# Group two's FFN: downs in seven products, sums of up weights stored ahead, squares of h moved

## The chip, the cores and the metric

The kernel runs on one core of a Trainium2 chip. The metric is the device time of one execution in microseconds; where several runs stand, the median counts. A core has five engines that run side by side, each with a queue of its own in program order: TensorE (PE), VectorE (DVE), ScalarE (ACT), GpSimd (POOL) and SyncE (SP), which only issues transfers. An instruction waits on semaphores for what it needs from other engines; all behind it in its queue wait with it.

## The reference

One layer of an encoder with two attention mixers and an FFN, for 1056 tokens (1024 of a prompt, 32 of a running stream), all in float32. The part that the change touches, cut down:

```python
h = x + jnp.einsum('bld,de->ble', m, w_out)
u = jnp.einsum('bld,df->blf', rmsnorm(h, g_ffn), w_up)        # 1024 -> 4096
return h + jnp.einsum('blf,fd->bld', jnp.square(jax.nn.relu(u)), w_down)
```

rmsnorm divides h by the root of the mean of its squares; since relu(u)^2 only scales with the square of that factor, the kernel uses h unscaled for the ups and multiplies the result by 1/(mean of squares + eps) at the end.

## The kernel before, in words

**Tiles.** Activations lie with channels on the 128 partitions and tokens along the columns. Each float32 operand is split in a high part, rounded to the fast matmul format, and the rest (`xh`, `xl`; `wh`, `wl`), and a block of 128x128 weights takes three matmuls (`three`: high times high, high times rest, rest times high). A *unit* is a 256 KB tile of weights, 128x512, four such blocks. For each unit SyncE loads `wst`, ACT casts it to `wh`, and POOL subtracts to get `wl` (`unit`, L435; three buffers for `wst`, five for each of the pair).

**Groups and stages.** The tokens are two groups: group one with 512, group two with 544 in two column halves of 272. Projections and most of the attention come first; then group one's output projection (`out`, L1325) and FFN (`ffn_group`, L1441: 16 ups, 32 downs by quarters `q` of the 4096 channels). Beside FFN one runs "late" attention of group two, which loads k, q and v of each head from DRAM (`k<-dk`, `q<-dq`, `v<-dv`). From about 1300 us on comes group two alone: branches, `out`, FFN two to the end.

**FFN two.** Its ups are already done by a seven-product scheme (Strassen's kind): two ups of 128 channels, two halves of the 1024 inputs and two halves of the columns make a 2x2 by 2x2 block product, which takes seven products of 12 matmuls of 128x272 instead of eight (`go_up_quad`, L1464). It needs four sums of weight tiles (`s1` to `s4`), made in FFN two itself: `quad_units` (L1389) loads a tile with SyncE and adds another one to it by an accumulating transfer, which only POOL's queue issues (four per quad, `raw<-w_up` on POOLq). The sums of h needed (`g.sums`) are made in `out`. The products add up in PSUM banks `pj`, DVE and ACT combine them, square the relu, and split the result. Downs are plain: `go_down` (L1511) takes one unit and two halves of 12 matmuls each into banks `pd`; DVE adds each to `y`. A quad of ups (84 matmuls) and four downs (96) take turns.

**Squares.** `out` also makes the sum of squares of h: for each of 8 row blocks ACT squares it, and POOL adds it to `acc` (L1345 to 1350); `scales` (L1446) sums that over partitions by a matmul with `ones` right after the first ups.

**Order.** All instructions are recorded first (`Plan.record`, L279), and a planner with a cost model then sets the order of each engine by rank and readiness (L353 to 416); all are issued at L410, so every row of the profile has that one line, and one tells groups apart by tile names and shapes.

Of the kernel before, what the change touches and what calls it, by code (L numbers as in the profile page):

```python
# [9 lines left out]
F32 = mybir.dt.float32  # L10
# [92 lines left out]
class Plan:  # L103
# [175 lines left out]
    def record(self, eng, fn, op, args, kw):  # L279
# [52 lines left out]
        if eng == SP and self.hold is not None:  # L332
            deps.add(self.hold)
# [85 lines left out]
class Layer:  # L419
# [77 lines left out]
    def run(self):  # L497
# [34 lines left out]
        self.dh = dt([KB, 128, T], "dh")  # L532

# [104 lines left out]
        self.ffn_group(g2)  # L638
# [640 lines left out]
    def begin_group(self, g, side):  # L1279
        nc, i = self.nc, g.i  # L1280
        g.pool = nc.open(f"g{i}", side)
        if i:
            g.h = nc.tile(g.pool, [128, KB, g.w], F32R, f"gh{i}")
            g.l = nc.tile(g.pool, [128, KB, g.w], F32R, f"gl{i}")
        g.y = nc.tile(g.pool, [128, KB, g.w], F32, f"y{i}")
        g.acc = [nc.tile(g.pool, [128, g.n], F32, f"acc{i}{c}") for c in range(len(g.chunks))]
        g.tmp = lambda name, tag, bufs: nc.tile(g.pool, [128, g.n], F32, name, tag=tag, bufs=bufs)
# [101 lines left out]
    def quad_units(self, f):  # L1389

        nc, a, w = self.nc, self.a, self.quads
        with nc.rank(PREP):
            src = lambda i, j: a["w_up"][f + i, j]

            def load(*blocks, out=None):
                st = out
                if out is None:
                    st = nc.tile(w, [128, 512], F32, "raw", bufs=10)
                    nc.sync.dma_start(st, src(*blocks[0]))
                    blocks = blocks[1:]  # L1400
                for b in blocks:
                    nc.gpsimd.dma_start(st, src(*b), accum_op=ALU.add)
                return st

            def part(z, pool, tag, bufs, eng):
                h = nc.tile(pool, [128, 512], F32R, tag + "h", bufs=bufs)
                l = nc.tile(pool, [128, 512], F32R, tag + "l", bufs=bufs)
                nc.scalar.copy(h, z)
                eng.tensor_sub(l, z, h.bitcast(F32))
                return h, l  # L1410

            V, G = nc.vector, nc.gpsimd
            z = load((1, 0), (1, 1))
            z3 = load((0, 0), (1, 0))
            a11, a22, a12 = load((0, 0)), load((1, 1)), load((0, 1))
            s1 = part(z, w, "s", 4, V)
            load((0, 0), out=z)
            s2 = part(z, w, "s", 4, V)
            load((0, 1), out=z)
            s3 = part(z3, w, "s", 4, V)  # L1420
            s4 = part(z, w, "s", 4, G)
            p11 = part(a11, self.wpool, "w", WB, G)
            p12 = part(a12, self.wpool, "w", WB, G)
            p22 = part(a22, self.wpool, "w", WB, G)
        return p11, p12, p22, s1, s2, s3, s4

    def square(self, g, ps, uh, ul, sign=1.0):

        nc = self.nc
        r = g.tmp("ru", "pb", 3)  # L1430
        nc.scalar.activation(r, ps, AF.Relu, scale=sign)
        if not g.i:
            nc.gpsimd.tensor_mul(r, r, r)
            nc.scalar.copy(uh, r)
            nc.vector.tensor_sub(ul, r, uh.bitcast(F32))
            return
        nc.vector.scalar_tensor_tensor(ps, ps, sign, r, op0=ALU.mult, op1=ALU.mult)
        nc.scalar.copy(uh, ps)
        nc.vector.tensor_sub(ul, ps, uh.bitcast(F32))

    def ffn_group(self, g, late=iter(())):  # L1441
        nc, a, i = self.nc, self.a, g.i
        n = g.n
        rb2 = g.acc

        def scales():  # L1446

            for c in range(len(g.chunks)):
                ps = self.bank("pj")
                nc.tensor.matmul(ps[:, :n], self.ones, g.acc[c], start=True, stop=True)  # L1450
                with nc.rank(FAST):
                    v = g.tmp("rv", "pb", 3)
                    nc.vector.tensor_scalar(v, ps[:, :n], 1.0 / D, EPS, op0=ALU.mult, op1=ALU.add)
                    nc.vector.reciprocal(rb2[c], v)

        nq, us = DFF // 512, {}

        def go_up(f):
            units = [self.unit(a["w_up"][f, j]) for j in range(2)]
            us[f] = uh, ul = g.mh[:, f % 8], g.ml[:, f % 8]  # L1460
            self.column_block(units, lambda k, cs: (g.h[:, k, cs], g.l[:, k, cs]),
                              lambda c, cs, ps: self.square(g, ps, uh[:, cs], ul[:, cs]), g.chunks)

        def go_up_quad(f):  # L1464

            a11, a12, a22, s1, s2, s3, s4 = self.quad_units(f)
            for i in range(2):
                us[f + i] = g.mh[:, (f + i) % 8], g.ml[:, (f + i) % 8]
            ta, tb, tc, td = ([(th[:, k], tl[:, k]) for k in range(4)] for th, tl in g.sums)
            x = lambda j, c: [(g.h[:, 4 * j + k, c * n:c * n + n], g.l[:, 4 * j + k, c * n:c * n + n]) for k in range(4)]  # L1470

            def product(w, xs, ps=None):
                first = ps is None
                if first:
                    ps = self.bank("pj")[:, :n]
                with nc.rank(FILL):
                    for k in range(4):
                        ks = slice(k * 128, k * 128 + 128)
                        self.three(ps, w[0][:, ks], w[1][:, ks], *xs[k], first and k == 0, k == 3, skip_group_check=True)
                return ps  # L1480

            def keep(ps):
                t = nc.tile(self.op, [128, g.w], F32, "part", tag="o32", bufs=4)[:, :n]
                with nc.rank(FAST):
                    nc.scalar.copy(t, ps)
                return t

            def done(i, c, out, ps, more=None):
                cs = slice(c * n, c * n + n)
                uh, ul = us[f + i]  # L1490
                with nc.rank(FAST):
                    if more is not None:
                        nc.vector.tensor_add(out, ps, more)
                    self.square(g, out, uh[:, cs], ul[:, cs], -1.0 if i else 1.0)

            px = product(a11, x(0, 0))
            p1 = keep(px)
            pz = product(s1, ta)
            p5 = keep(pz)
            product(s2, tb, px)  # L1500
            u2 = keep(px)
            product(s4, x(1, 1), pz)
            done(0, 1, pz, pz, u2)
            py = product(a12, x(1, 0))
            done(0, 0, py, py, p1)
            product(s3, tc, px)
            done(1, 1, self.bank("pj")[:, :n], px, p5)
            product(a22, td, px)
            done(1, 0, px, px)

        def go_down(e, q):  # L1511
            units = [self.unit(a["w_down"][e, q])]

            def done(c, cs, ps):
                y = g.y[:, e, cs]
                if q == 0:
                    nc.scalar.copy(y, ps)
                    return
                if q < nq - 1:
                    nc.vector.tensor_add(y, ps, y)  # L1520
                    return
                if e < KB // 2:
                    nc.vector.tensor_add(ps, ps, y)
                    y = hx_of(e, cs)
                nc.vector.tensor_mul(ps, ps, rb2[c])
                nc.vector.tensor_add(g.y[:, e, cs], ps, y)
                nc.sync.dma_start(self.o["yT"][:, e, slice(g.lo + cs.start, g.lo + cs.stop)], g.y[:, e, cs])

            if q == nq - 1 and e >= KB // 2:
                for c, cs in enumerate(g.chunks):  # L1530
                    y = g.y[:, e, cs]
                    nc.gpsimd.tensor_mul(y, y, rb2[c])
                    nc.gpsimd.tensor_add(y, y, hx_of(e, cs))
            self.column_block(units, lambda k, cs: (us[4 * q + k][0][:, cs], us[4 * q + k][1][:, cs]), done, g.chunks,
                              kn=4, tag="pd" if g.i else "pj")

        def hx_of(e, cs):

            return g.h.bitcast(F32)[:, e, cs]

        def reload():

            with nc.rank(PREP):
                nc.sync.dma_start(g.h.bitcast(F32), self.dh[:, :, g.lo:g.lo + g.w].rearrange("e p t -> p e t"))
# [14 lines left out]
        if g.i:  # L1559
            go_up_quad(0)  # L1560
            scales()
            go_up_quad(2)
            for q in range(nq):
# [103 lines left out]
```

## Time and profile before

| | us |
|---|---|
| runs | 1767.86, 1769.7, 1771.3 (median 1769.7) |
| profiled execution, its own time | 1771.3 |
| its span in the trace | 1769.5 |
| start of FFN two | about 1393 |
| last matmul | 1765.5 |
| mean granted clock of TensorE | 0.999 |

Tile names: `gh`, `gl` are h times the norm's gain in its two parts; `xh`, `xl` sums or results that were split; `sh`, `sl` split weight sums; `ru` relu; `part` a kept partial product; `acc` the sum of squares. A row of a group of instructions gives its line, engine, operation, tiles and shapes, the count, busy time and mean nanoseconds of one, then the engine's idle time ahead of them and what ended it.

### The profile page before, as it was taken

The numbers are of one execution on the slowest core, as the hardware profiler recorded it, in microseconds if no ns is written. First come the engines' busy times: TensorE is split into PE (matmuls) and PEld (weight loads), VectorE is DVE, ScalarE is ACT, GpSimd is POOL, SyncE is SP. The second block draws the span as 40 slices with busy tenths as digits, with TensorE's granted clock in tenths as the row PEclk, the third lists the DMA queues.
The fourth block names the chain that finished last, engine by engine and source line by source line (L and its number), as shares of the span: only waits on it lengthen the run. The fifth ranks groups of instructions, "written<-read, shape, count | busy, mean of one in ns | idle before, by whom it ended". The sixth has DMA issues, their size and how long they took to land.

```text
span 1769.5 us, 32605 instructions
## 1 busy us (share of the span) xinstructions
PE 1741.2 (98%) x11394; PEld 1599.9 (90%) x11394; DVE 1050.6 (59%) x2284; ACT 976.5 (55%) x2153; POOL 1046.0 (59%) x909
## 2 busy tenths in 40 slices
PE   8999999999999999999999999999999999999999
PEld 7999999999889888988888888888899999999998
DVE  7555578999655644888755455222347843444445
ACT  7444598983255776766665555533236654444441
POOL 3623232435366575999864555665759966666555
PEclk9999999999999999999999999999999999999999
DMA  7243451444566668556344453533486576666634
GB/s 255 74 133 117 116 177 59 147 144 143 178 173 169 177 183 228 172 177 179 100 135 127 125 144 96 156 101 96 155 262 191 153 169 150 151 153 156 154 68 137
DMA packets 169908, 264.53 MB, mean 149 GB/s; under 512 B 28944, under 2 KB 58224, under 8 KB 169744
## 3 DMA queue, kind: packets, MB, share of 16 engines
q1 hardware_dynamic: 160096, 245.33, 47.3%
q0 software_dynamic: 9216, 16.78, 5.9%
q8 instruction: 90, 1.47, 0.4%
q14 instruction: 74, 0.61, 0.1%
q10 hardware_dynamic: 432, 0.34, 0.1%
HBM read 207.87 MB, written 54.40 MB: 148 GB/s over the span
## 4 chain that ended last, share of the span: by engine, by line
PE 85%; DMA 4%; POOL 4%; DVE 3%; issue 2%; ACT 1%; SPq 1%; ACTq 0%; POOLq 0%; DVEq 0%
PE pj L410 52%; PE s L410 13%; PE pd L410 11%; PE t L410 5%; PE o L410 5%; POOL wl L410 1%; DMA wst<-w_ba 1%; SPq L410 1%; DVE xl L410 1%; POOL xl L410 1%; POOL pb L410 1%; POOL acc L410 0%; DMA raw<-w_up 0%; DMA wst<-w_g 0%; DMA xt<-x 0%
## 5 line engine op out<-in xcount | busy, mean ns | idle before, releaser
L410 POOL TENSOR_TENSOR wl<-wst,wh 128x512 fp32r<-128x512 f32 x350 | 485.7, 1395 | 357.2 <-ACT wh L410 324.6
L410 PE MATMUL pj<-xh,wh 128*128 128x512 f32 (+1 forms) x1600 | 557.2, 349 | 0.7 <-DVE vt L410 0.3
L410 PE MATMUL pj<-xh,wl 128*128 128x512 f32 (+1 forms) x1600 | 557.5, 349 | 0.0
L410 PE MATMUL pj<-xl,wh 128*128 128x512 f32 (+1 forms) x1600 | 555.9, 348 | 0.1
L410 ACT CAST wh<-wst 128x512 fp32r<-128x512 f32 x350 | 216.9, 621 | 327.9 <-PE pj L410 167.4
L410 PEld LDWEIGHTS pj<-xh,wh 128*128 128x128 f32 x1600 | 300.8, 188 | 34.0 <-ACT xh L410 1.0
L410 PEld LDWEIGHTS pj<-xh,wl 128*128 128x128 f32 x1600 | 300.8, 188 | 32.9
L410 PEld LDWEIGHTS pj<-xl,wh 128*128 128x128 f32 x1600 | 301.0, 188 | 32.7 <-DVE xl L410 0.3
L410 PE MATMUL pd<-xh,wh 128*128 128x272 f32 x512 | 147.9, 289 | 2.1 <-ACT y L410 1.8
L410 PE MATMUL pd<-xl,wh 128*128 128x272 f32 x512 | 147.6, 288 | 0.0
L410 PE MATMUL pd<-xh,wl 128*128 128x272 f32 x512 | 147.6, 288 | 0.0
L410 DVE TENSOR_TENSOR tt<-t,tt 128x512 fp32r<-128x512 f32 (+2 forms) x168 | 100.5, 624 | 48.6 <-ACT tt L410 46.8
L410 DVE TENSOR_TENSOR_SCAN rem<-rem 128x896 f32<-128x896 f32 (+6 forms) x66 | 118.3, 1816 | 10.5 <-ACT rem L410 10.1
L410 ACT ACTIVATE junk<-score,cand 128x384 bf16<-128x384 f32 (+1 forms) x124 | 116.1, 936 | 9.8 <-DVE cand L410 7.8
L410 POOL TENSOR_TENSOR p<-p,rem 128x895 f32<-128x895 f32 (+6 forms) x66 | 100.9, 1541 | 30.3 <-DVE rem L410 25.3
L410 ACT CAST tt<-t 128x512 fp32r<-128x512 f32 (+2 forms) x168 | 84.6, 541 | 39.1 <-PE t L410 35.2
L410 PE MATMUL s<-wl,xh 128*128 128x256 f32 (+1 forms) x360 | 101.8, 286 | 0.2 <-POOL wl L410 0.2
L410 PEld LDWEIGHTS o<-tt,v 128*128 128x128 f32 x640 | 92.7, 188 | 9.5 <-ACT wh L410 0.8
L410 PE MATMUL s<-wh,xh 128*128 128x256 f32 (+1 forms) x360 | 100.3, 286 | 0.9 <-DVE small L410 0.8
L410 PE MATMUL s<-wh,xl 128*128 128x256 f32 (+1 forms) x360 | 100.8, 283 | 0.0
L410 PE MATMUL s<-k,q 128*128 128x384 f32 (+5 forms) x384 | 95.8, 356 | 4.7 <-DMA k<-dk 2.0
L410 PEld LDWEIGHTS pd<-xh,wh 128*128 128x128 f32 x512 | 96.5, 189 | 3.3 <-ACT y L410 2.0
(260 smaller groups left out, 3847.9 us busy)
## 6 DMA issues: line engine op xcount, KB each, us to landing
wst<-w_down SPq DMA_DIRECT2D x128, 256.0 KB, 2.7
raw<-w_up SPq DMA_DIRECT2D x80, 256.0 KB, 3.2
q<-dq SPq DMA_DIRECT2D x64, 256.0 KB, 5.2
wst<-w_up SPq DMA_DIRECT2D x64, 256.0 KB, 2.7
raw<-w_up POOLq DMA_DIRECT2D x64, 256.0 KB, 4.6
k<-dk SPq DMA_DIRECT2D x48, 256.0 KB, 3.5
v<-dv SPq DMA_DIRECT2D x48, 256.0 KB, 3.6
wst<-w_g SPq DMA_DIRECT2D x42, 256.0 KB, 3.4
```

The lines of the kernel that those rows point to most:

```text
L410: fn(*args, **kw)
```

## The change

1. FFN two gets a function of its own, `ffn_quads`: four ups, then four downs for each quarter, both in seven products of 12 matmuls. All products use the six `pj` banks; the two `pd` banks hold weight sums.
2. Sums of down weights are made by DVE in PSUM from four loaded tiles: three adds into a `pd` bank, one in SBUF.
3. Sums of up weights are made during FFN one in DRAM, 16 tensors of 1 MB: a copy from ACT's queue and an accumulating transfer from POOL's queue for each, spread by `tick` over 18 places. In FFN two SyncE loads seven tiles for an up, and no transfer accumulates.
4. Squares of h move out of `out` to behind the first up, in place and over both halves at once; `scales` moves to the start of the third quarter of FFN one and to behind the fifth up of FFN two.
5. Weights of up and down lie in DRAM in another order, and a buffer turn (`turn`) puts loads in nine slots and split weights in seven.

The diff, cut to its core:

```diff
-        if eng == SP and self.hold is not None:
+        if op == "dma_start" and self.hold is not None:
             deps.add(self.hold)
...
+    def weight_sums(self):
+        nc, a = self.nc, self.a
+        held = []
+        def add(out, src):
+            nc.gpsimd.dma_start(out, src, accum_op=ALU.add, max_dma_last_dim=8192)
+        for (w, q), s in self.sums.items():
+            w11, w12, w21, w22 = (a[w][i, 4 * q:4 * q + 4].rearrange("t (a b) c -> (t a) (b c)", b=4) for i in range(4))
+            s1, s2, s3, s4 = s
+            for out, src, more in ((s1, w21, w22), (s3, w11, w21), (s2, w11, s1), (s4, w12, s2)):
+                nc.scalar.dma_start(out, src)
+                held.append((out, more))
+                if len(held) > 2:
+                    add(*held.pop(0))
+                yield
+        for x in held:
+            add(*x)
+            yield
+
+    def tick(self):
+        with self.nc.rank(SLOW), self.nc.behind():
+            next(self.steps, None)
...
-                if e == 0:
-                    nc.scalar.activation(g.acc[c], hv, AF.Square)
-                else:
-                    sq = g.tmp("sq", "pb", 3)
-                    nc.scalar.activation(sq, hv, AF.Square)
-                    nc.gpsimd.tensor_add(g.acc[c], g.acc[c], sq)
...
+    def squares(self, g):
+        for e in range(KB):
+            y = g.y[:, e]
+            if e == 0:
+                self.nc.scalar.activation(g.ss, y, AF.Square)
+            else:
+                self.nc.scalar.activation(y, y, AF.Square)
+                self.nc.gpsimd.tensor_add(g.ss, g.ss, y)
...
+        def down_weights(q, i):
+            src = [a["w_down"][p, 4 * q + i] for p in range(4)]
+            with nc.rank(PREP):
+                w11 = load(src[0])
+                wt = pair(w11, G)
+            yield wt
+            with nc.rank(PREP):
+                w21, w22 = load(src[2]), load(src[3])
+                z = self.bank("pd")
+                add(z, w21, w22)
+                wt = pair(z, V)
+            yield wt
+            with nc.rank(PREP):
+                add(z, z, w11)
+                wt = pair(z, V)
+            yield wt
+            with nc.rank(PREP):
+                w12 = load(src[1])
+                add(z, z, w12)
+                wt = pair(z, V)
+            yield wt
+            for z, y, eng in ((w21, w11, G), (w12, None, G), (w22, None, G)):
+                with nc.rank(PREP):
+                    if y is not None:
+                        add(z, z, y)
+                    wt = pair(z, eng)
+                yield wt
...
+        def up(q, j):
...
+            py = product(next(wt), x[5])
+            with nc.rank(FAST):
+                add(py, py, p1)
+                square(py, py, 1.0)
+                parts(U11[j], py, V)
+                sub(t1, py, u12)
+                parts(T1[j], t1, G)
+                V.scalar_tensor_tensor(t2, t1, -1.0, pw, op0=ALU.mult, op1=ALU.subtract)
+                parts(T2[j], t2, G)
+            product(next(wt), x[6], px)
...
+        def down(q, i):
...
+            px = product(next(wt), u[0])
+            gather(0, 0, px, 1.0, 0)
+            pz = product(next(wt), u[1])
+            gather(1, 1, pz, -1.0, 0)
+            product(next(wt), u[2], px)
+            gather(0, 1, px, 1.0, 0)
+            product(next(wt), u[3], pz)
+            gather(0, 1, pz, 1.0, 1)
+            product(next(wt), u[4], px)
+            gather(1, 1, px, -1.0, 1)
+            py = product(next(wt), u[5])
+            gather(0, 0, py, 1.0, 1)
+            product(next(wt), u[6], px)
+            gather(1, 0, px, -1.0, 2)
+
+        for q in range(4):
+            for j in range(4):
+                up(q, j)
+                if q + j == 0:
+                    self.squares(g)
+                if q == 1 and j == 0:
+                    self.scales(g)
+            if q == 3:
+                self.reload(g)
+            for i in range(4):
+                down(q, i)
...
         go_up(0)
-        scales()
+        self.squares(g)
         for q in range(nq):
+            if q == 2:
+                self.scales(g)
             for f in range(4 * q + 1, min(4 * q + 5, 4 * nq)):
                 go_up(f)
+                if f >= 5 and f % 3:
+                    self.tick()
                 beside(2)
```

`product` is the loop of 12 matmuls that stood in `go_up_quad`; `pair` casts a loaded tile on ACT and subtracts on the engine named (G is POOL, V is DVE); `gather` adds a product to `y` or subtracts it, and in the last quarter scales by `acc`, adds h and stores.

Three places show what moves in the queues. First TensorE in the downs of FFN two (names: `pd` and `pj` are PSUM tiles, `wh`, `wl`, `sh`, `sl` weights, `xh1`, `uh` results of the ups). Before, two downs stand there so (the first rows of each half):

```order
L410 MATMUL pd_16011<-xh1_94,wh_16009 128x272 [waits DVE_49]
...
L410 MATMUL pd_16011<-xh1_94,wl_16010 128x272 [waits Pool_49]
...
L410 MATMUL pd_16012<-xh1_94,wh_16009 128x272 [waits DVE_49]
...
L410 MATMUL pd_16016<-xh1_94,wh_16014 128x272 [waits DVE_49]
...
L410 MATMUL pd_16016<-xh1_94,wl_16015 128x272 [waits Pool_49]
...
L410 MATMUL pd_16017<-xh1_94,wh_16014 128x272 [waits DVE_49]
```

Each half has a bank of its own. After, a down of the second quarter stands there so (the first row of each of its seven products and, where it waits, of a weight rest):

```order
L410 MATMUL pj_16176<-xh1_110,wh_16174 128x272 [waits Activation_49]
...
L410 MATMUL pj_16176<-xh1_110,wl_16175 128x272 [waits Pool_49]
...
L410 MATMUL pj_16181<-xh1_110,wh_16179 128x272 [waits Activation_49]
...
L410 MATMUL pj_16176<-xh1_110,wh_16182 128x272 [waits DVE_49,Activation_49]
...
L410 MATMUL pj_16181<-xh1_110,wh_16185 128x272 [waits DVE_49,Activation_49]
...
L410 MATMUL pj_16176<-uh_15776,sh_16187 128x272 [waits DVE_49]
...
L410 MATMUL pj_16191<-uh_15776,sl_16190 128x272 [waits Pool_49]
...
L410 MATMUL pj_16176<-uh_15776,wh_16192 128x272 [waits DVE_49,Activation_49]
```

Products 3, 4, 5 and 7 return to a bank, `pj_16176` or `pj_16181`, that a gather has read in the meantime, with 12 matmuls of another bank between.

Second, POOL at FFN two's entry. Before, its queue has weight rests, the adding transfers (`DMA raw<-w_up`), and the last of the squares:

```order
L410 TENSOR_TENSOR acc_14403<-acc_14403,sq 128x272 [waits Pool_49]
L410 DMA raw<-w_up 128x512 [waits DMASW2_49,DVE_49]
L410 TENSOR_TENSOR wl<-raw,wh 128x512 [waits PE_49] x2
...
L410 DMA raw<-w_up 128x512 [waits DMAHW4_49,DMASW3_49,DVE_49]
L410 DMA raw<-w_up 128x512 [waits DMASW0_49,DVE_49]
L410 TENSOR_TENSOR wl<-wst,wh 128x512 [waits PE_49,Activation_49]
```

After, during the ups behind the first, weight rests and squares stand there, and `xl_111`, two rests of the results for the downs; no transfer does:

```order
L410 TENSOR_TENSOR acc_14508<-acc_14508,y_14507 128x544
L410 TENSOR_TENSOR wl<-wst,wh 128x512 [waits DMAHW5_49,PE_49,Activation_49]
L410 TENSOR_TENSOR acc_14508<-acc_14508,y_14507 128x544 [waits Pool_49]
L410 TENSOR_TENSOR sl<-wst,sh 128x512 [waits DMAHW2_49,PE_49,Activation_49]
L410 TENSOR_TENSOR acc_14508<-acc_14508,y_14507 128x544 [waits Pool_49] x2
L410 TENSOR_TENSOR xl_111<-ut,xh_110 128x272 [waits Activation_49]
```

The squares' adds moved behind the entry, and the transfers are gone from it.

Third, POOL in FFN one after (`p<-p,nb` belongs to the late attention, `ru` to the ups, `dw_up` are the sums in DRAM):

```order
L410 TENSOR_TENSOR wl<-wst,wh 128x512 [waits DMAHW2_49,PE_49,Activation_49]
L410 DMA dw_up_89<-dw_up_87 128x2048 [waits DMASW2_49]
L410 TENSOR_TENSOR ru<-ru 128x512 [waits Activation_49]
L410 TENSOR_TENSOR wl<-wst,wh 128x512 [waits DMAHW3_49,PE_49,Pool_49]
L410 TENSOR_SCALAR p<-p,nb 128x768 [waits DVE_49]
L410 TENSOR_TENSOR wl<-wst,wh 128x512 [waits PE_49,DMAHW4_49,Activation_49,Pool_49]
L410 DMA dw_up_90<-w_up 128x2048
```

The two transfers are new; an add whose addend is itself a sum (`dw_up_87`) waits for the add that made it.

More of the change, by code (lines that the diff above doesn't have):

```diff
@@ L532, in run @@
         self.dh = dt([KB, 128, T], "dh")
+        self.sums = {(w, q): [dt([128, 2048], f"d{w}{q}{i}") for i in range(4)] for w in ("w_up",) for q in range(4)}
+        self.steps = self.weight_sums()
         self.wpool = nc.open("w")
@@ L1285, in begin_group @@
         g.y = nc.tile(g.pool, [128, KB, g.w], F32, f"y{i}")
[L1286 removed]
+        g.ss = nc.tile(g.pool, [128, g.w], F32, f"acc{i}")
+        g.acc = [g.ss[:, cs] for cs in g.chunks]
         g.tmp = lambda name, tag, bufs: nc.tile(g.pool, [128, g.n], F32, name, tag=tag, bufs=bufs)
@@ L1387, in quarters @@
             part(3, t4)
[L1389 to L1425, printed above, removed]
@@ L1441, in ffn_group @@
[L1441 to L1483, printed above, removed]
@@ new lines, in squares, with scales @@
+    def squares(self, g):
[6 more added lines that the diff above has]
+                self.nc.gpsimd.tensor_add(g.ss, g.ss, y)
+    def scales(self, g):
+        nc = self.nc
+        for c in range(len(g.chunks)):
+            ps = self.bank("pj")
+            nc.tensor.matmul(ps[:, :g.n], self.ones, g.acc[c], start=True, stop=True)
+            with nc.rank(FAST):
+                v = g.tmp("rv", "pb", 3)
+                nc.vector.tensor_scalar(v, ps[:, :g.n], 1.0 / D, EPS, op0=ALU.mult, op1=ALU.add)
+                nc.vector.reciprocal(g.acc[c], v)
@@ new lines, in reload, with finish @@
+    def reload(self, g):
+        with self.nc.rank(PREP):
+            self.nc.sync.dma_start(
+                g.h.bitcast(F32), self.dh[:, :, g.lo:g.lo + g.w].rearrange("e p t -> p e t"))
+    def finish(self, g, e, c, cs, ps, sign=1.0):
+        nc = self.nc
+        y = g.y[:, e, cs]
+        nc.vector.tensor_mul(ps, ps, g.acc[c])
+        (nc.vector.tensor_add if sign > 0 else nc.vector.tensor_sub)(y, y, ps)
+        nc.sync.dma_start(self.o["yT"][:, e, slice(g.lo + cs.start, g.lo + cs.stop)], y)
@@ L1497, in go_up_quad, with square @@
[L1497 to L1509, printed above, removed]
+            def square(out, ps, sign):
+                r = g.tmp("ru", "pb", 3)
+                nc.scalar.activation(r, ps, AF.Relu, scale=sign)
+                V.scalar_tensor_tensor(out, ps, sign, r, op0=ALU.mult, op1=ALU.mult)
@@ new lines, in up @@
+            px = product(next(wt), x[0])
+            keep(p1, px)
+            pz = product(next(wt), x[1])
+            keep(p5, pz)
+            product(next(wt), x[2], px)
+            keep(u2, px)
+            product(next(wt), x[3], pz)
+            with nc.rank(FAST):
+                add(pz, pz, u2)
+                square(u12, pz, 1.0)
+            product(next(wt), x[4], px)
+            pw = turn("bank", banks)
+            with nc.rank(FAST):
+                add(pw, px, p5)
+                square(pw, pw, -1.0)
+                parts(U22[j], pw, V)
+                sub(pz, pw, u12)
+                parts(T3[j], pz, V)
@@ new lines, in ffn_quads, with ffn_group, source, go_up @@
+        for q in range(4):
[5 more added lines that the diff above has]
+                    self.scales(g)
+            if q == 3:
+                self.reload(g)
+            for i in range(4):
+                down(q, i)
+    def ffn_group(self, g, late=iter(())):
+        nc, a = self.nc, self.a
+        nq, us = DFF // 512, {}
+        def source(name, row, col, t):
+            return a[name][2 * row + col, t]
+        def go_up(f):
+            units = [self.unit(source("w_up", f % 8 // 4, j, 4 * (f // 8) + f % 4)) for j in range(2)]
+            us[f] = uh, ul = g.mh[:, f % 8], g.ml[:, f % 8]
+            def done(c, cs, ps):
+                r = g.tmp("ru", "pb", 3)
+                nc.scalar.activation(r, ps, AF.Relu)
+                nc.gpsimd.tensor_mul(r, r, r)
+                nc.scalar.copy(uh[:, cs], r)
+                nc.vector.tensor_sub(ul[:, cs], r, uh.bitcast(F32)[:, cs])
+            self.column_block(units, lambda k, cs: (g.h[:, k, cs], g.l[:, k, cs]), done, g.chunks)
@@ L1585, in ffn_group @@
                 beside(1)
+        for _ in self.steps:
+            pass
 def _host_arrays(inp):
```

162 lines of the change are left out of this document (108 added, 54 removed).

## The prediction

> **What bounds the kernel now.** I read the page from the top: the span, the busy shares, the shares of the chain that ended last.
>
> ```profile
> span 1769.5 us, 32605 instructions
> PE 1741.2 (98%) x11394; PEld 1599.9 (90%) x11394; DVE 1050.6 (59%) x2284; ACT 976.5 (55%) x2153; POOL 1046.0 (59%) x909
> PE 85%; DMA 4%; POOL 4%; DVE 3%; issue 2%; ACT 1%; SPq 1%; ACTq 0%; POOLq 0%; DVEq 0%
> ```
>
> TensorE is busy 98% of the span and 85% of the chain; no other engine passes 59%. The profiled execution took 1771.3 us, 1.8 us of it outside its span, and stands 1.6 us above the median of 1769.7. Next the windows of group two's part, from its output projection (1360) to the end (columns: window, length, then busy time and instructions of PE, PEld, DVE, ACT, POOL, then clock, DMA share, GB/s).
>
> ```profile
> 1360.00:1396.00 36.00, 36.00 (x288) 36.00 (x287) 27.54 (x33) 24.63 (x57) 36.00 (x36) 1.00 0.60 184
> 1408.00:1441.00 33.00, 29.19 (x216) 28.46 (x215) 19.06 (x36) 17.33 (x44) 19.14 (x18) 0.95 0.76 167
> 1416.80:1420.20 3.40, 3.40 (x17) 3.40 (x17) 0.45 (x1) 1.29 (x3) 3.00 (x3) 0.50 0.83 187
> 1500.00:1700.00 200.00, 200.00 (x1597) 200.00 (x1596) 86.40 (x196) 90.02 (x196) 121.22 (x106) 1.00 0.63 143
> ```
>
> From 1500 to 1700 TensorE never stops: 200 us / 1597 = 125.2 ns for each matmul of 128x272, at full clock, with DVE at 43%, ACT 45%, POOL 61%. There the time is the count of matmuls. Only the entry, 1408 to 1441, loses time. TensorE's waits from 1300 to the end are these five, and the timeline has the two large ones (start, length, instruction, idle before):
>
> ```profile
> PE pj L410 <- DVE sl L410: 2.0, 1, 2.0
> PE pd L410 <- ACT y L410: 1.8, 1, 1.8
> PE pj L410 <- DVE pb L410: 1.2, 1, 1.2
> PE pj L410 <- DVE y L410: 1.1, 1, 1.1
> PE pj L410 <- POOL acc L410: 0.7, 2, 0.5
> ```
> ```profile
> 1413.87 0.29 PE L410 MATMUL pj<-gh,wl 128*128 128x272 f32 x1
> 1416.14 0.39 PE L410 MATMUL pj<-gh,sl 128*128 128x272 f32 x1 [1.99 <-DVE sl L410]
> ...
> 1438.77 0.29 PE L410 MATMUL pd<-xh,wl 128*128 128x272 f32 x1
> 1440.88 0.40 PE L410 MATMUL pd<-xh,wh 128*128 128x272 f32 x1 [1.82 <-ACT y L410]
> ```
>
> **The change, part by part.**
>
> *Downs in seven products.* Before, a cycle of FFN two is one up (7 products of 12 matmuls, 84) and four downs of 24, 180 in all; the chain of waits shows its period:
>
> ```profile
> 1514.69 8.92 PE pj L410 x71
> ...
> 1537.27 8.92 PE pj L410 x71
> ```
>
> 22.58 us / 180 = 125.4 ns, the same rate. Four such downs become one of 84, 16 times: 16 x 12 = 192 matmuls fewer. At 125.2 ns: **-24.0 us**.
>
> *The entry.* Before, the sums of up weights are made in FFN two by adding transfers behind POOL's queue. The chain shows one of them ahead of the second stall:
>
> ```profile
> 1431.35 0.88 POOL raw L410
> 1432.26 7.30 DMA raw<-w_up
> ```
>
> After, the sums lie ready in DRAM and SyncE loads them plainly. The stalls at 1413.87 (2.27 us from start to start, less 0.125: 2.15) and at 1438.77 (2.11 less 0.125: 1.98) lose their cause, and the wait for acc (0.7) goes with the squares. The windows show clock 0.50 for 3.40 us after the first stall, which cost half, 1.7. Together **-6.5 us**; bounds 0 (another load is late instead) and -6.5. I take it whole: SyncE's loads land sooner than the adding ones (3.2 and 2.7 below, against 7.30 here).
>
> The half clock began after a wait of only 2.15 us. The Trainium skill ("TensorE: Matmul & The Clock Gate", Part 1) says that the clock halves after at least one idle window of about 3.4 us; by that the wait did not cause it, and the sum would be smaller by 1.7 us. The trace, where the slow stretch starts 0.7 us behind this wait and nowhere else in FFN two, speaks for the wait.
>
> *What the other engines must now do in an up and a down.* 168 matmuls are 21.0 us. Groups of instructions by form (busy, mean ns):
>
> ```profile
> L410 DVE TENSOR_TENSOR y<-pj,y 128x512 f32<-128x512 f32 x60 | 41.4, 690 | 70.0 <-PE pj L410 69.5
> L410 DVE TENSOR_TENSOR y<-pd,y 128x272 f32<-128x272 f32 x104 | 45.9, 442 | 69.8 <-PE pd L410 69.0
> L410 DVE TENSOR_TENSOR sl<-raw,sh 128x512 fp32r<-128x512 f32 x48 | 37.1, 791 | 58.1 <-ACT sh L410 58.0
> L410 ACT CAST wh<-wst 128x512 fp32r<-128x512 f32 x350 | 216.9, 621 | 327.9 <-PE pj L410 167.4 <-PE pd L410 66.0 <-issue 51.5
> L410 ACT CAST xh<-pj 128x272 fp32r<-128x272 f32 x64 | 24.3, 381 | 1.0 <-DVE pj L410 1.0
> L410 POOL TENSOR_TENSOR wl<-raw,wh 128x512 fp32r<-128x512 f32 x48 | 63.4, 1342 | 13.0 <-ACT wh L410 12.9
> L410 POOL TENSOR_TENSOR xl<-raw,xh 128x272 fp32r<-128x272 f32 x12 | 11.0, 943 | 0.0
> L410 POOL TENSOR_TENSOR acc<-acc,sq 128x272 f32<-128x272 f32 x14 | 12.1, 870 | 0.0
> ```
>
> DVE: an up has 16 operations on 272 columns at 0.44 and 2 weight rests at 0.79, 8.6 us; a down 4 weight sums and 3 rests at about 0.7 (nearest row: 0.69, from PSUM) and 7 gathers at 0.44, 8.0. Sum 16.6 of 21.0, 79%; with the 2 sums that read SBUF alone at twice 0.79 it would be 18. ACT: 14 weight casts at 0.62 and 14 small ones at 0.38, 14.0, 67%. POOL: 9 weight rests at 1.34 and 2 small ones at 0.94, 14.0, 67%. All stay below TensorE, DVE with the least room. The last four downs have 14 DVE operations of 272 instead of 7, about 11 us for 10.5 of matmuls; that they lag there is worth a microsecond or two.
>
> *New waits in the downs.* Products 3, 4, 5 and 7 of a down accumulate on a bank that DVE or ACT has just read. Between the last matmul of the product in that bank and the first of the next stand 12 matmuls (1.5 us), and a read is 0.38 to 0.44; so 1.0 us is left for a DVE queue that holds at most one weight sum (0.69). Behind the waiting matmul the whole of TensorE's queue stands. 64 such places: nothing when the read is at the head of its queue; 0.375 us each would eat the 24.0. Before, a unit's accumulate and read were not coupled like this; the nearest case is the ups of FFN two, whose products are coupled to DVE and ACT in the same way, and none of the five waits above begins after 1438.77. So near nothing: **+2 us**, bounds 0 and +24. At the four places where downs follow the last up, 30 matmuls (3.75 us) stand between that up's sixth product and the first use of its result, whose chain of four short operations takes about 1.7: nothing to **+1**.
>
> *Squares of h* leave the output projection, where POOL was busy 36.00 of 36.00 us (14 adds x 0.87 = 12.2 us off it), and come as 7 adds on double width (about 1.7 each, again 12 us) among the first ups' weight rests, where POOL has 10.5 - 8.6 = 1.9 us free per up. Their result is needed only at the fifth up. Cover is the weights prepared ahead; if it is gone, the adds cost up to 12 - 4 x 1.9 = 4.6 us once. I take 0, as with the 8 squares of ACT (0.38 x 2 each).
>
> *Transfers in FFN one.* 16 copies of 1 MB from ACT's queue and 16 adds of 1 MB from POOL's are new, while the first half of FFN one runs beside the late attention heads of group two. The page's DMA row of 40 slices, its queues and its issues:
>
> ```profile
> DMA  7243451444566668556344453533486576666634
> ...
> q1 hardware_dynamic: 160096, 245.33, 47.3%
> q0 software_dynamic: 9216, 16.78, 5.9%
> ...
> raw<-w_up SPq DMA_DIRECT2D x80, 256.0 KB, 3.2
> q<-dq SPq DMA_DIRECT2D x64, 256.0 KB, 5.2
> wst<-w_up SPq DMA_DIRECT2D x64, 256.0 KB, 2.7
> ```
>
> q1: 245.33 MB in 47.3% of 1769.5 is 837 us, 3.6 us per 1 MB. q0: 16.78 MB in 104 us, 6.5 us per 1 MB. In all 16 x 10.1 = 162 us of engine time (estimates). The DMA row (slices of 44 us) stands at 3 to 5 tenths from 840 to 1280, which is FFN one but its first part; 162 us over these 440 add under 4 tenths, so the total has room. One transfer may delay a load it meets. Weights are covered: SyncE's issue of them already waits 299.9 us for buffers to come free (row below), so they arrive early. The q, k and v of a head are not: in the timeline the last q load goes out at 1050.91 and the first matmul on it starts at 1059.00, 8.1 us, of which landing is 5.2.
>
> ```profile
> SPq L410 <- POOL wl L410: 299.9, 116, 7.7
> ```
> ```profile
> 1050.91 1.24 SPq L410 DMA_DIRECT2D q<-dq  x2
> ...
> 1059.00 1.29 PE L410 MATMUL s<-k,q 128*128 128x448 f32 x5
> ```
>
> About 3 us of margin. By the program's order some 7 heads still load their q while copies and adds run. Bounds: 0, or 7 heads x (3.6 + 6.5 + 5.2 - 3 = 12.3) = 86. The nearest row is SyncE loads beside accumulating ones, 3.2 against 2.7: half a microsecond, inside the margin. I take **+3** for one or two unlucky heads. ACT's and POOL's issue time (0.9 us per add by 0.88 above) falls on engines with over 40% free.
>
> The Trainium skill ("DMA: Bandwidth & Descriptors", Queues, rings and completion order) has each DMA engine go round robin between its queues, a packet at a time, which speaks against the change: with three queues at work a q load would get a third. No run so far shows it for transfers of 1 MB; by it the sum would be that of the slower rival below.
>
> *Sum:* -24.0 - 6.5 + 2 + 1 + 3 = -24.5; from 1771.3 to 1746.8, and from the median to 1745.2. The tail behind the last matmul is unchanged.
>
> **The rivals.**
>
> *Downs paced by the other engines.* DVE's 79% bunches: sums, gathers and the ups' squares share one queue in order, and weights prepared two or three ahead run out. For it: the ladder of DVE sums ahead of products 2 to 4. Against: 20% free and seven pairs of weight buffers. At 0.2 us for each of 64 gated products, +13: about 1757.
>
> *Transfers hold the attention heads of FFN one.* Half of the 12.3 us for two or three of the 7 heads, +15 - 3: about 1757.
>
> *Slower than before.* The same mechanism, at all heads, if a q load shares the engines evenly with a copy and an add: it lands in 3 x 5.2 = 15.6 us, 10.4 late, 7.4 past the margin, and 7 heads make 52: about 1745 - 3 + 52 = 1794. It decides from (24.5 + 3) / 7 = 3.9 us per head. Against: beside accumulating transfers SyncE's loads lost only the half microsecond above. The even share is the rule of the Trainium skill cited above ("DMA: Bandwidth & Descriptors", Queues, rings and completion order).
>
> *It gains more.* FFN one loses nothing, and FFN two runs without a wait (-6), and POOL's relief takes the two waits of 1.2 and 1.1 us in the output projection (-2.3): about 1737.
>
> *The change doesn't do what it says*, and the time stays: the count of matmuls falls by 192 by the program's own order, so this could only be the first rival at 0.375 us per product.
>
> **How the numbers follow.** Forecast 1739 to 1750: 0.62. Downs paced 0.15; heads held 0.10; slower 0.07; more gained 0.06. The predicted time is 1745. The range 1736 to 1758 takes in the first two rivals and the gain, and leaves out the slower case and the far ends of the others. A measurement can tell about 0.2%, 3.5 us: faster 0.90, same 0.03, slower 0.07.
>
> **What would show it.** Right: in FFN two about 200 matmuls per 25 us without idle rows, 192 fewer in all, no half clock at the entry, the span of the late attention as before. Downs paced: rows of TensorE waiting for DVE y, ACT y or DVE pd in FFN two. Heads held: TensorE waiting for a DMA of q, k or v, with q's landing above 5.2. Wrong altogether: an engine other than TensorE above 90% from 1400 on.

## The result, and the profile after

The changed kernel takes 1783.41 us (median of six runs, 1779.48 to 1791.09) against 1770.97 for the one before, a ratio of 1.0075 with an interval of 1.0059 to 1.0091. It is slower by 0.75%, where 1745 and "faster" were forecast, and the time lies outside the range. (One passage above is wrong, though nothing was worked out from it: FFN one has 32 ups and 64 downs in eight steps `q`, not 16 and 32 by quarters; its `scales` moved to the start of the third of these eight.)

The page of the changed kernel, the lines that answer to those of before (span; busy us, share and instructions of each engine; queues with packets, MB and share):

```profile
span 1777.3 us, 32637 instructions
PE 1729.1 (97%) x11202; PEld 1580.7 (89%) x11202; DVE 1123.2 (63%) x2448; ACT 1018.8 (57%) x2241; POOL 1057.7 (60%) x894
...
q1 hardware_dynamic: 164704, 253.72, 47.7%
q0 software_dynamic: 2304, 16.78, 4.8%
q10 hardware_dynamic: 944, 17.12, 2.5%
```

The 192 matmuls are gone and TensorE is 12 us less busy, but the span is 7.8 us longer. TensorE runs the same number of matmuls in both kernels up to FFN two, so the starts of matmuls by their number tell where the time went (profiled executions, us from the span's start):

| matmul | before | after | difference |
|---|---|---|---|
| 4860, just ahead of group one's output projection | 737.2 | 738.1 | +0.9 |
| 7741, last of FFN one | 1293.4 | 1317.2 | +23.9 |
| 8500, end of group two's output projection | 1392.8 | 1412.8 | +20.0 |
| last | 1765.5 | 1773.3 | +7.9 |

FFN one, here with the output projection ahead of it, lost 23.0 us, the branches and the output projection gained 3.9, and from 8500 on the kernel gained 12.2. TensorE's waits in the changed kernel between 1100 and 1310 us, the second half of FFN one (engine and tile, who released it: us, times, longest):

```profile
PE pj L410 <- ACT wh L410: 10.9, 5, 3.7
PE pj L410 <- POOL wl L410: 2.3, 4, 0.7
PE pj L410 <- DVE y L410: 1.8, 1, 1.8
PE s L410 <- issue: 1.3, 1, 1.3
```

Before, no wait of TensorE stood in that stretch (1100 to 1310); its releasers now are the casts and rests of weights. One of them in the timeline, around 1200 us: ACT, then TensorE.

```profile
1191.91 0.50 ACTq L410 DMA_DIRECT2D dw_up<-w_up  x1
...
1197.27 0.50 ACTq L410 DMA_DIRECT2D dw_up<-w_up  x1
...
1209.32 0.62 ACT L410 CAST wh<-wst 128x512 fp32r<-128x512 f32 x1 [9.69 <-DMA wst<-w_down]
```
```profile
1210.00 0.50 PE L410 MATMUL pj<-xh,wh 128*128 128x512 f32 x1 [1.89 <-ACT wh L410]
```

Two adds go out at 1190.99 and 1198.92 beside these two copies. The weights of 256 KB that SyncE asks for in the same stretch land late; asked tile by tile, the trace has for the five loads of `wst` from 1188 to 1204, after the change, this answer first; the second is that of the kernel before for all its 52 loads of `wst` from 1150 to 1290:

```profile
L410 SPq DMA_DIRECT2D wst<-w_down x5: 328/328/328, 1189.4 to 1201.1; - x5
...
DMA to landing us min/median/max: 2.6/11.3/15.2
```
```profile
DMA to landing us min/median/max: 2.4/2.6/7.2
```

A load of 2.6 us takes up to 15.2, ACT idles 9.69 us for it, and TensorE waits.

The packets in the trace show how the engines share their time there. A load moves in packets of 2 KB that take 0.10 us, an add in packets of 8 KB that take 0.63, a copy in packets of 64 KB that take 2.4. From 1205 to 1210 us the 16 DMA engines move 95 packets of the add issued at 1198.92 and 107 of loads, evenly mixed. So loads and adds take turns nearly packet for packet, but the loads get 9.5 us of the 75 that these packets take. The loads issued at 1194.82 and 1196.52, ahead of that add, land at 1209.25 and 1211.74 among its packets: these two were held by a transfer issued behind them as well.

Past FFN two's entry, which is as clean as forecast, TensorE waits in short pieces. All of them from 1400 on that reach 0.9 us:

```profile
PE pj L410 <- ACT xh L410: 3.4, 5, 2.0
PE pj L410 <- DVE ul L410: 1.4, 2, 1.0
PE pj L410 <- ACT wh L410: 1.3, 3, 0.6
PE pj L410 <- DVE xl L410: 1.0, 2, 0.8
PE pj L410 <- ACT part L410: 1.0, 2, 0.6
PE pj L410 <- DVE pj L410: 0.9, 1, 0.9
```

From 8500 on 2702 matmuls take 360.5 us where 125.2 ns each make 338.3: 22 us are lost, in waits, slow starts behind them, and two stretches at half clock (windows: clock stands third from the end):

```profile
1465.10:1468.50 3.40, 3.40 (x17) 3.40 (x16) 3.13 (x6) 1.32 (x4) 2.01 (x2) 0.50 0.33 82
1560.70:1564.10 3.40, 3.40 (x17) 3.40 (x17) 2.88 (x7) 0.78 (x3) 0.72 (x1) 0.51 0.29 81
```

### The profile page after: what moved, and what is told of

Same layout as the page of the kernel before. It is cut to its first block, busy times and chain, and to the rows that moved or that the text cites. A ratio compares the mean times of both kernels' runs of the same rounds, so it can differ in the third digit from the quotient of the medians.

```text
span 1777.3 us, 32637 instructions
## 1 busy us (share of the span) xinstructions
PE 1729.1 (97%) x11202; PEld 1580.7 (89%) x11202; DVE 1123.2 (63%) x2448; ACT 1018.8 (57%) x2241; POOL 1057.7 (60%) x894
## 5 line engine op out<-in xcount | busy, mean ns | idle before, releaser
L410 PE MATMUL pj<-xh,wh 128*128 128x272 f32 (+1 forms) x1920 | 654.5, 342 | 19.2 <-ACT wh L410 11.7
L410 PE MATMUL pj<-xh,wl 128*128 128x272 f32 (+1 forms) x1920 | 652.5, 341 | 2.3 <-POOL wl L410 2.3
L410 PE MATMUL pj<-xl,wh 128*128 128x272 f32 (+1 forms) x1920 | 652.6, 340 | 1.5 <-DVE xl L410 1.0
L410 PEld LDWEIGHTS pj<-xh,wh 128*128 128x128 f32 x1920 | 363.4, 189 | 57.7 <-ACT wh L410 16.4
L410 PEld LDWEIGHTS pj<-xh,wl 128*128 128x128 f32 x1920 | 363.4, 189 | 37.9 <-POOL wl L410 4.2
L410 PEld LDWEIGHTS pj<-xl,wh 128*128 128x128 f32 x1920 | 363.9, 190 | 34.6 <-DVE xl L410 1.4
L410 DVE TENSOR_TENSOR y<-pj,y 128x512 f32<-128x512 f32 (+1 forms) x104 | 59.4, 572 | 98.7 <-PE pj L410 98.2
L410 PE MATMUL o<-tt,v 128*128 128x256 f32 (+1 forms) x640 | 98.8, 276 | 0.0
L410 PE MATMUL pj<-gh,wh 128*128 128x272 f32 x320 | 92.7, 290 | 1.3 <-DVE rv L410 0.7
L410 PE MATMUL pj<-gh,wl 128*128 128x272 f32 x320 | 92.3, 289 | 0.7 <-DVE wl L410 0.7
```

The lines of the kernel that those rows point to most:

```text
L410: fn(*args, **kw)
```

## The experiments

Two questions: do the 1 MB transfers cost FFN one its 23 us, and by what (bytes, size, rows, adds or copies); and what costs FFN two its 22? In the tables "FFN one" is the time from matmul 4860 to 7741, so it takes in the output projection ahead of it (556.2 before, 579.1 after), "FFN two" that from 8500 to the last (360.5 after). These come from one profiled execution of each kernel, times and ratios from all runs, each against the kernel before on the same chip.

**e1: no transfers.** The ups of FFN two load single tiles in place of the four sums, as many loads of the same size.

```diff
-        self.steps = self.weight_sums()
+        self.steps = iter(())
...
+            s1, s2, s3, s4 = w22, w12, w11, w22
```

> The changed kernel without the 16 copies and 16 adds in FFN one; the ups of group two load single tiles of w_up in place of the four sums (as many loads of the same size), so group two's output leaves the sums out. Theory T (the 1 MB transfers hold SyncE's weight loads in FFN one; matmul 7741, the last of FFN one, starts at 1317.2 instead of 1293.4): that start falls back to 1293 within 2 us, the time to 1783 - 24 = about 1759. Rival R (the moved squares and scales and the planner's changed order cost it): the start stays near 1317 and the time near 1783.

1757.77 us, ratio 0.9919 (0.9897 to 0.9941). FFN one takes 555.0; TensorE has no wait between 1100 and 1310. Theory T holds to about a microsecond in the time: the transfers cost about 25 us, the moved squares and scales nothing in FFN one. Matmul 7741 starts at 1296.4, 1.4 us later than expected, and that much and more was lost ahead of matmul 4860 (741.4 against 738.1).

**e2: the kernel before with the transfers alone** (`weight_sums`, `tick` and its places added).

> The kernel before with nothing but the 16 copies and 16 adds of 1 MB, at the same places of FFN one; nothing reads the sums. Theory T: FFN one ends 20 to 25 us later than before, 1771 + 24 = about 1795, with waits of ACT wh for wst loads that land in over 10 us. Rival R: within 3 us of 1771.

1821.78 us, ratio 1.0285 (1.0263 to 1.0308): +51, twice the expectation. FFN one takes 604.9. Here heads are hit too (matmul 7000 starts at 1151.6 against 1125.4):

```profile
PE s L410 <- issue: 11.4, 2, 9.0
PE s L410 <- DMA q<-dq: 8.2, 2, 6.7
PE pj L410 <- ACT wh L410: 7.4, 3, 2.8
```

The sign is T's. Why the same transfers cost twice as much in this kernel, whose order of instructions is another, no run shows.

**e3: the same transfers early, e4: without the down sums.** e3 moves the ticks from FFN one into the loops of projections; e4 is e3 without the weight sums of the downs on DVE (single tiles are split in their place).

```diff
             self.index_projection(1, s)
+            self.tick()
...
-                if f >= 5 and f % 3:
-                    self.tick()
```

> The changed kernel with the same copies and adds issued earlier, one at a time beside the projections (some 50 to 450 us), where the DMA share before is 0.3 to 0.5. Theory T: there the loads have more lead (the four index and q/k/v projections use a tile for many tokens), so FFN one ends as before and the time is that of e1, about 1759, or up to 10 more if the projections wait for loads now. Rival R: near 1783. Rival S (the transfers cost their 20 us wherever they run, since loads wait behind them everywhere): near 1780 with the loss before 450 us.

1800.24 us, ratio 1.0165 (1.0143 to 1.0188): worse than in FFN one. FFN one takes 555.4, but matmul 4000 starts at 651.5 instead of 599.9. Nine copies and three adds go out between 61 and 95 us, and a weight load waits behind them:

```profile
105.64 0.62 ACT L410 CAST wh<-wst 128x512 fp32r<-128x512 f32 x1 [10.45 <-DMA wst<-w_vb]
```
```profile
107.58 0.69 PE L410 MATMUL s<-kih,qi 128*128 128x384 f32 x1 [4.86 <-DVE score L410]
```

That cast stands in ACT's queue ahead of the relus of the scores, for which DVE and then TensorE wait. A low DMA share (0.30 to 0.53 before) was no cover. It is rival S, and more than its price.

> e3 with the four weight sums of each down left out (single tiles are split in their place), so that DVE has about 4 us less to do in each of 16 downs; the output of group two leaves the sums out. FFN two loses 22 us against 125.2 ns for each of its matmuls after the change. Theory D (DVE's weight sums collide with the last up's splits at the turn from ups to downs): 10 to 18 us less than e3, the waits at the four turns gone. Rival G (products wait for the gathers of their bank): within 4 us of e3.

1792.32 us against e3's 1800.24. FFN two takes 350.0 in place of 360.6: of its 22 us about 10 hang on DVE's weight sums, as theory D has it; its figure of 10 to 18 holds in the profile, and by the medians it is 8.

**f1: copies alone; f3: copies in 8 KB rows.** f1 empties `add`; f3 gives the copy `max_dma_last_dim=8192`.

> The changed kernel with the 16 copies of 1 MB from ACT's queue, without the 16 adds from POOL's (the sums stay single tiles; group two's output leaves the second addend out). Without both the time is 1758, with both 1783. Theory A (the adds, which take 10 to 14 us each, hold the weight loads behind them): within 4 us of 1758. Theory C (the copies in 64 KB rows hold them): within 5 us of 1783. If each only hurts beside the other: about 1758 too, with single loads of 5 to 8 us.

1759.34 us, ratio 0.9928 (0.9906 to 0.9950); FFN one 557.9. Copies alone cost 1.6 us against e1 by the medians, 2.9 in FFN one by the profiles.

> The changed kernel with each copy of 1 MB in 128 rows of 8 KB instead of 16 of 64 KB, as the adds are; nothing else. Theory P (a load waits for whole 64 KB rows ahead of it in a DMA engine): loads beside copies land in under 6 us, time about 1765. Theory B (it waits for the bytes of what was issued ahead, whatever the rows): within 4 us of 1783.

1781.88 us, ratio 1.0063 (1.0045 to 1.0082): no different from the change (its profiled execution, at 1787.83 the slowest of its eight, shows 586.0 in FFN one). The length of a row doesn't matter: a copy of 1 MB is now 128 packets of 0.31 us instead of 16 of 2.4, so the engines are about as long at it.

**f4: pieces of 256 KB.**

```diff
-                nc.scalar.dma_start(out, src)
-                held.append((out, more))
+                for i in range(4):
+                    ps = slice(32 * i, 32 * i + 32)
+                    nc.scalar.dma_start(out[ps], src[ps], max_dma_last_dim=8192)
+                    held.append((out[ps], more[ps]))
```

with one tick after each down and two after each up, so that the pieces are used up half way.

> The changed kernel with each copy and each add cut in four pieces of 256 KB, 64 and 64, spread one by one over the ups and downs of FFN one; same bytes, same result. Theory S (a load is late by the size of the single transfer that it meets, about 12 us for 1 MB, so 3 for 256 KB, less than the weights' lead): FFN one ends near 1296, time about 1760. Theory V (the bytes moved cost the same however cut): about 1783. Rival (64 issues of 0.9 us in POOL's queue and more waits there cost): 1765 to 1775 with waits for POOL wl.

1779.16 us, ratio 1.0040 (1.0028 to 1.0052). It looks like theory V, but the place of the loss moved: FFN one takes 574.6, of which 19 us are lost between 900 and 1000 us, where up to nine pieces go out in 10 us (loads of 10 to 14 us), and next to nothing from 1100 to 1155, with six or seven in 10 us and no bunch of heads' loads beside them, and later, when all are done. From 1100 to 1155 weights land in up to 9.4 us, and the work that lies ready covers it.

**g1: sums into SBUF in FFN two**, by adding transfers of 256 KB as before the change.

> The changed kernel without sums in DRAM: the four sums of up weights are made in FFN two as before the change, by adding transfers of 256 KB into SBUF from POOL's queue (four per up); all else as changed, complete result. FFN one then ends near 1296 as in e1. If FFN two bears the 64 issues (0.9 us each in POOL's queue, and the chain split, add, split): e1's 1758 plus 0 to 8, clearly faster than before. If POOL becomes the bound there (14.0 + 3.6 = 17.6 of 21 us by durations, with waits): 1770 or more.

1791.71 us, ratio 1.0110 (1.0090 to 1.0131). Ahead of FFN two nothing is lost, but from 8500 on 2702 matmuls take 398 us. POOL is not full there (265 of 390 us); weights come late through the chain of split, add, split, which TensorE feels as waits for `wh` (14.8 us in 11 waits). Arranged like this, FFN two with downs in seven products has no room for the sums.

**h1: the pieces spread over all of FFN one**, one step after each up and each second down.

> The changed kernel with pieces of 256 KB again (64 copies, 64 adds), but one step after each up and after each second down of FFN one instead of three times as many, so that they reach over all of FFN one; in f4 they were in flight four to six at once beside the first heads (adds of 7 us, loads of 10 to 14 us there, 19 us lost before matmul 6500) and cost nothing after it, where two or fewer met. Theory Q (a load is late by what is in flight ahead of it): FFN one ends within 5 us of 1296, time 1757 to 1764. Rival V (the bytes cost the same however cut and spread): about 1780.

1763.53 us, ratio 0.9962 (0.9946 to 0.9978); FFN one 561.5. The same bytes, in the same pieces as in f4, cost 13 (FFN one) to 16 us (medians) less when spread, as theory Q expected. The loads of `wst` issued from 1150 to 1268.5 land no later than this:

```profile
DMA to landing us min/median/max: 2.5/4.1/6.8
```

Three behind them, from 1269.5 on, take 10 to 13 us, and TensorE waits 2.19 us at 1282. From 1100 to 1280 it idles 0.2 us:

```profile
1100.00:1280.00 180.00, 179.84 (x824) 149.74 (x822) 57.57 (x83) 69.22 (x120) 137.38 (x124) 1.00 0.79 209
```
```profile
1100.00:1300.00 200.00, 183.68 (x816) 149.26 (x815) 52.92 (x86) 70.51 (x120) 124.77 (x105) 0.99 0.76 217
```

The first row is h1, the second the changed kernel: the DMA share is the same (0.79 and 0.76), and TensorE loses nothing in one and 16 us in the other. The mean share doesn't tell them apart, the pile does: in the changed kernel the packets fill all 16 engines from 1199 to 1210 us (176 us of packet time in 16 times 11).

**h4: copies early, only adds in FFN one.**

> The changed kernel with its 16 copies of 1 MB issued early, beside the projections, and only the 16 adds of 1 MB left in FFN one. Copies alone (f1) cost 1.5 us of the 25. If the adds alone hold the loads: FFN one loses its 20 us as changed, near 1780. If it takes a copy and an add side by side: FFN one ends near 1300 and the time is 1758 to 1766, loads beside an add landing in 5 to 8 us.

1772.72 us, ratio 1.0014 (1.0001 to 1.0028). FFN one takes 565.1: against e1's 555.0 adds alone cost 10 us there, copies alone (f1) 3, both 24. Alone the adds land in 8.6 and 9.2 us (medians of both kinds) instead of 13.0 and 11.0. Both expectations were half right. The early copies cost 9 us ahead of matmul 4000, so the total says little.

**h2: scales among the downs.** `scales(g)` goes from behind the fifth up to behind the second down of the second quarter.

> h1 with group two's scales (two sums by ones, two reciprocals of 1.85 us on DVE) moved from behind the fifth up to between two downs of the second quarter. In the changed kernel TensorE loses 3.6 us in four waits around them. Theory D (DVE has room in the downs, not among the ups' splits): 3 to 4 us less than h1. Rival (the loss moves along): within 1.5 us.

1755.98 us, ratio 0.9922 (0.9899 to 0.9945); 7.5 less than h1, twice the expectation; FFN two 352.6 against 361.9. Around the scales the changed kernel shows on DVE:

```profile
1517.80 1.84 DVE L410 RECIPROCAL acc<-rv 128x272 f32<-128x272 f32 x1
1519.56 0.38 DVE L410 TENSOR_TENSOR xl<-pj,xh 128x272 fp32r<-128x272 f32 x1
```

and 30 us later, at the turn from ups to downs of that quarter, DVE, then TensorE:

```profile
1548.74 1.42 DVE L410 TENSOR_TENSOR wst<-wst 128x512 f32<-128x512 f32 x1
...
1551.72 1.41 DVE L410 TENSOR_TENSOR pd<-raw 128x512 f32<-128x512 f32 x1
1553.06 0.42 DVE L410 TENSOR_TENSOR ul<-pj,uh 128x272 fp32r<-128x272 f32 x1
1553.41 0.78 DVE L410 TENSOR_TENSOR pj<-pj,part 128x272 f32<-128x272 f32 x2
```
```profile
1554.24 0.39 PE L410 MATMUL pj<-xh,wh 128*128 128x272 f32 x1 [0.92 <-DVE pj L410]
1557.99 0.71 PE L410 MATMUL pj<-xh,wh 128*128 128x272 f32 x2 [1.98 <-ACT xh L410]
```

In h2 both places are free but for 1.05 us. So the two reciprocals of 1.84 us cost the waits beside them. The turn, where weight sums stand between the last up's operations, gained as well, and its half clock is gone, but not simply because DVE was still behind from the scales: in the changed kernel it idles in between, last for over a microsecond here.

```profile
1541.88 0.69 DVE L410 TENSOR_TENSOR sl<-raw,sh 128x512 fp32r<-128x512 f32 x1 [1.12 <-ACT sh L410]
```

With the scales moved the planner also set the rows of the turn in another order; no run separates this from the scales themselves.

**h3, i1, i2: squares and the last bunch.** h3 is h2 with the squares back in `out`; i1 is h2 with six more steps, so that no pieces are left to bunch behind FFN one; i2 is i1 with the squares back.

> h2 with group two's squares of h back in its output projection (16 squares on ACT, 14 adds on POOL), as before the change. If their 7 adds of 128x544 on POOL and 8 squares on ACT behind the first up cause the first turn's waits (about 3 us of TensorE at the turn from ups to downs in the first quarter and a half clock of 1.7): 3 to 5 us less than h2. If the turn's waits are DVE's weight sums alone: the first turn keeps its waits, and the time is that of h2 or up to 3 more, since the output projection's POOL is full.

1754.91 us, ratio 0.9902 (0.9869 to 0.9936), within h2's spread; FFN two 348.5 against 352.6.

> h2 with six more steps in FFN one, so that no pieces are left to run in a bunch behind its last down (in h2 five adds and four copies lie between 1300 and 1320, and TensorE waits 1.5 us at 1279 and 0.9 at 1319). If the bunch causes these two: 1753 to 1755, 2 us less than h2. If it is only where the weights of the last quarter are short: 1755 to 1758.

1756.13 us, ratio 0.9919 (0.9893 to 0.9946): no better than h2. The wait at 1319 is gone, the one before 1280 is still there (2.3 us lost). A miss for the bunch. The time is its rival's, whose cause, weights short in the last step, isn't shown: DVE's `y` ends the wait.

> i1 with group two's squares back in its output projection, as h3. In h3's trace FFN two took 4.1 us less than in h2 but the stretches ahead of it 7 more, of which 5 lie before matmul 4000, where the kernels do not differ. Theory (the squares cost 4 us at the first turn and nothing in the output projection): 3 to 4 us less than i1. Rival (what the turn gains is lost in the projection): within 1.5 us of i1.

1752.13 us, ratio 0.9889 (0.9876 to 0.9902); FFN two 350.9 against i1's 353.7. The squares cost 3 to 4 us by the profiles; by the times the intervals of i1 and i2 meet, so it isn't more than likely. i2 is the fastest complete kernel here: 19 us below the one before, 31 below the change. Its FFN two still takes 12.6 us more than its matmuls at 125.2 ns (338.3). The gains of e4 (10) and h2 (9) lie in part at the same turn and can't be added; what is left of the 22 no run takes apart.

| kernel | time | FFN one | FFN two |
|---|---|---|---|
| after | 1783.4 | 579.1 | 360.5 |
| e1, no transfers | 1757.8 | 555.0 | 360.9 |
| f4, pieces bunched | 1779.2 | 574.6 | 361.4 |
| h1, pieces spread | 1763.5 | 561.5 | 361.9 |
| h2, and scales moved | 1756.0 | 560.5 | 352.6 |
| i2, and squares back | 1752.1 | 560.4 | 350.9 |

## Why the prediction was wrong, by its own steps

*Count of matmuls, -24.0:* right; 192 are gone, and e1 with the same FFN two stands 12.4 us below the kernel before even with FFN two's losses.

*Entry, -6.5:* right. No wait of before is left there, the half clock at 1416.8 is gone, and from matmul 8500 to 8850 the changed kernel takes 46.0 us instead of 52.4. The output projection gained 3.9, which was put in the rival of a larger gain at 2.3.

*Transfers in FFN one, +3:* this is the step that failed: "Weights are covered: SyncE's issue of them already waits 299.9 us for buffers to come free (row below), so they arrive early." It cost 23.0. A queue that waits for buffers is ahead by as many buffers as there are, and no more: their lead held loads of 2.6 us, and in h1 of up to 6.8, not several in a row of up to 15.2. The price was in the prediction itself, 12.3 us for a load that meets a copy and an add, but it was applied to the heads alone. They lost little: by matmul 7040, past the last head in both kernels, the change was 1.4 us behind. The slower rival had the mechanism and the wrong victim; its chance of 0.07 rested on the 0.5 us that loads lose beside single 256 KB adds, a row that doesn't carry over to 1 MB. Beside spread pieces of 256 KB (h1) loads lose 1.5 us at the median (4.1 against 2.6), three times that price, but the lead covers it.

*New waits in the downs, +2 and +1:* mis-sized; from 8500 on the gain was 12.2 instead of 27.5 (24.0 + 6.5 - 3). The weight lay on the wrong place. The 64 products behind a gather, which got the +2, hardly wait; what waits are the turns, which got +1, and the scales, which got nothing: there DVE has the ups' splits, weight sums and reciprocals at once (e4, h2). The working took DVE's 79% as a mean over up and down and never set the scales' two reciprocals anywhere. The weight sums were a little short too: the 32 that read both tiles from SBUF took 0.67 to 1.79 us, 1.02 in the mean, against 0.7 assumed, which puts an up and a down at about 17.3 us of DVE (estimate), between the 16.6 and the 18 of the working.

*Squares, 0 (bounds to 4.6):* 3 to 4 by h3 and i2, inside the bounds.

*The two rules of the Trainium skill.* On queues ("DMA: Bandwidth & Descriptors", Queues, rings and completion order): each DMA engine goes round robin between its queues, a packet at a time. Taken as an even share among three queues, that would make a load of 2.6 us one of 7.8 (estimate); 11.3 in the middle and 15.2 at most were measured beside two adds and two copies. The trace agrees with turns by packet, 95 to 107 above, but not with an even share: a turn of 0.63 us against one of 0.10 left the loads an eighth of the time. So the rule did speak against the change, by more than the prediction made of it. On the clock ("TensorE: Matmul & The Clock Gate", Part 1): here too half clocks of 3.4 us follow waits shorter than the window the page gives, such as the one of 1.98 us before 1560.7; the 1.7 us was rightly put down to the wait.

## What to carry to other kernels

Before adding large transfers beside a stage that is fed by small loads, compare the lead of those loads, in us of work that lies ready in buffers, with the landing time of what will be in flight ahead of them; a free DMA share is no answer. Compare their packets too: a load that takes turns with longer ones gets little of the engines' time. Cut the transfers to the size of the loads and space them; in h1 two were in flight on average between 1155 and 1290 us, four at most. When an engine's share rises to 80%, look for the places where two of its tasks fall together (a turn between phases, a slow single operation), and put slow ones where the other task pauses.

## What the hardware showed that was not expected

Copies and adds together cost FFN one 24 us where apart they cost 3 and 10. A load issued within 0.1 us of an add is not held (2.6 us for the one at 1191.07, issued 0.08 behind an add), since the add's first packet starts only at 1193.03; those 3 us later are (14.4). And waits of about 2 us cost nearly twice their length where a half clock of 3.4 or 6.8 us follows: the changed kernel has 17 us of it ahead of its last matmul, the one before 3.4; but not each does, as the waits of 1.89 and 0.67 us at 1210 were followed by full clock. The half clocks start on a grid: those of the changed kernel at 1174.9, 1297.8, 1465.1 and 1560.7, which is 36, 49 and 28 times 3.413 us apart, and the same step fits all 16 profiles. From 30 us on, the clock was halved behind every step of that grid with over 1.95 us of idle TensorE (by the profile, where the ends of matmuls are modelled), and no half clock began behind one with under 1.0; in between, both happen. The 1.89 us at 1210 were split over two steps (0.93 and 0.96).
